# Storing normalized tokens in quarters: one edit in the input projection of a hybrid mixer kernel

## The chip, the cores and the metric

The kernel runs on one core of one Trainium2 chip. The metric is device time in microseconds (us) of one execution; a lower time is better. The core has TensorE (PE, matrix products; its weight loads are shown as PEld), VectorE (DVE), ScalarE (ACT), GpSimd (POOL) and SyncE (SP). SP computes nothing here: it issues nearly all DMA transfers, in the order of its own queue, and an issue whose data aren't ready holds everything that is queued behind it.

## What is computed

Two layers, each over 2048 latent tokens and 256 context tokens of width 1024. A layer normalizes its tokens, modulates them, projects them once for four parallel mixers (differential attention, an S5 state space model, a gated linear recurrence HGRN2, and multi-head latent attention), gates the mixers' outputs, projects them back and adds them to the residual:

```
shift, scale, gate = jnp.split(mod.astype(F32), 3, axis=-1)
h = (rms_norm(x) * (1.0 + scale) + shift).astype(dt)
(da_q, da_k, da_v, da_g, s5_u, s5_g, hg_q, hg_ff, hg_fb, hg_i, hg_g,
 mla_cq, mla_ckv, mla_kr, mla_g) = split_columns(h @ P["w_in"][l])
...
mixed = jnp.concatenate([a_out, b_out, c_out, d_out], axis=-1)
x = (x.astype(F32) + gate * (mixed @ P["w_out"][l]).astype(F32)).astype(dt)
```

All data are float32. `h`, the normalized tokens, is what this case is about.

## The kernel before, in words

A layer runs in three phases: the first stage, the mixers, and the output projection. The 2304 tokens (2048 latent, then 256 context) stand in the free dimension, the width in eight chunks of 128 partitions. Products of full precision are made of three passes over a high and a low part of each operand (`mm3`, lines 176 to 179): high times high, high times low, low times high.

The first stage of a layer is `proj1`, woven with `s5_build`, which works out the tables of the S5 mixer on GpSimd, VectorE and ScalarE and some on TensorE (`first_stage`). `proj1` cuts the tokens into six parts of 384. For each part `prep` (line 432) calls `h_block` (line 275): three token tiles are loaded, squared and summed on ScalarE, and for each of the eight chunks TensorE transposes and scales them (line 299), ScalarE writes the high part `hi` (line 304) and the unrounded value `t32` (line 305), and VectorE writes the low part `lo` as their difference (line 306). High and low part are tiles of 128 partitions by 8 chunks by 384 tokens, 1536 KB each. Parts 0, 2, 4 share one pair of buffers and parts 1, 3, 5 another.

`proj1` itself needs the parts only in those buffers. It multiplies them with five blocks of weights for attention keys and queries, and with value weights, and its evacuations (`evac1`, `store_qk` line 356, values line 501) store to memory: `KD` and `QD` take the keys and queries of differential attention, `KRD` the shared rotary key, `VT` the values. The second projection, `proj2`, works in blocks of 576 tokens, and loads `h` back from the tensor `HD` (line 522). `keep` (line 439) is what puts it there: one store of the whole high part and one of the whole low part (line 441).

`keep(0)` is called behind the loads of all weights, `keep(1)` behind the fourth block of weights of part 0, and every other one right after its `prep`. The program is written in this order, but a planner with durations of its own works out the order of each engine's queue and of SP's from it (`schedule_with_timeline_sim` in `TCKW`): instructions are placed when their operands are ready by its clock, the earlier written first. In layer 0 the first part is prepared while the modulation is worked out (`startup`), whose sixteen weight loads go through seven buffers.

The S5 build stores its tables `SC` (lines 1303 and 1312) and `ED` (line 1335) from the same SP queue. When it ends, its space goes to `proj2`, whose first four loads of `h` follow then.

Of the kernel before, what the change touches and what calls it, by code (L numbers as in the profile page):

```python
# [10 lines left out]
F32 = mybir.dt.float32  # L11
# [92 lines left out]
def run(g):  # L104
    for _ in g:
        pass


PR = (0, 0)
AVB = 2  # L110
PPB = 3
DA_A = 740
# [32 lines left out]
def pst(g, tag, name):  # L145
    if tag == "mm":
        tags = g.banks.get(name, g.banks["*"])
        g.rr[name if name in g.banks else "*"] += 1
        tag = tags[g.rr[name if name in g.banks else "*"] % len(tags)]
    return g.ps.tile([128, 512], F32, tag=tag, name=name, bufs=PSB[tag])  # L150


def pool(g, name, bufs, side="left"):
    return g.tc.tile_pool(name=name, bufs=bufs, side=side, reuse_waits="tile")
# [31 lines left out]
def rsqrt_col(g, pool, out, ss, inv_n, tag):  # L186
    nc = g.nc
    v = pool.tile([128, 1], F32, tag=tag + "v", name=tag + "v")
    nc.vector.tensor_scalar(v, ss, inv_n, EPS, ALU.mult, ALU.add)
    nc.gpsimd.tensor_tensor(out, v, g.mhalf, ALU.pow)  # L190
# [78 lines left out]
def x_src(g, l, tok):  # L269
    if l == 0:  # L270
        return g.A["x_s"][tok:tok + 128] if tok < LS else g.A["x_p"][tok - LS:tok - LS + 128]
    return g.X1[tok:tok + 128]


def h_block(g, l, tok0, n, p, hi, lo, mod):
    nc = g.nc
    xs, ds = [], []
    for t in range(n // 128):
        xt = p.tile([128, D], F32, tag="xt", name="xt", bufs=3)
        nc.sync.dma_start(xt, x_src(g, l, tok0 + t * 128))  # L280
        ss = p.tile([128, 1], F32, tag="ss", name="ss")
        junk = p.tile([128, D], BF16, tag="junk", name="junk", bufs=1)
        nc.scalar.activation(out=junk, in_=xt, func=AF.Square, accum_out=ss)
        r = p.tile([128, 1], F32, tag="r", name="r")
        rsqrt_col(g, p, r, ss, 1.0 / D, "rs")
        dg = p.tile([128, 128], F32, tag="dg", name="dg", bufs=4)
        nc.vector.tensor_scalar(dg, g.ident, r, None, ALU.mult)
        xs.append(xt)
        ds.append(dg)
    cut = min(max(LS - tok0, 0), n)  # L290
    if mod is not None:
        next(mod)
    for kc in range(8):
        if mod is not None and kc % 2 == 0:
            next(mod)
            next(mod)
        ps = pst(g, "mm", "pst")
        for t in range(n // 128):
            nc.tensor.matmul(ps[:, t * 128:(t + 1) * 128], lhsT=xs[t][:, kc * 128:(kc + 1) * 128], rhs=ds[t], start=True, stop=True)
        t32 = p.tile([128, 384], F32, tag="t32", name="t32")  # L300
        for a, b, gr in ((0, cut, 0), (cut, n, 1)):
            if b > a:
                sc, sh = g.scale[:, gr, kc:kc + 1], g.shift[:, gr, kc:kc + 1]
                nc.scalar.activation(out=hi[:, kc, a:b], in_=ps[:, a:b], func=AF.Identity, bias=sh, scale=sc)
                nc.scalar.activation(out=t32[:, a:b], in_=ps[:, a:b], func=AF.Identity, bias=sh, scale=sc)
        nc.vector.tensor_tensor(lo[:, kc, :], t32, hi[:, kc, :].bitcast(F32), ALU.subtract)
    if mod is not None:
        run(mod)

# [111 lines left out]
def proj1(g, l):  # L421
    nc = g.nc
    N = 384
    with ExitStack() as es:
        px = es.enter_context(pool(g, "pjx", 2))
        ph0 = es.enter_context(pool(g, "pjh0", 1))
        pw0 = es.enter_context(pool(g, "pjw0", 1))
        pws = es.enter_context(pool(g, "pjs", 2))
        starts = list(range(0, NT, N))
        hs = {}  # L430

        def prep(i):
            ph = ph1 if i % 2 else ph0
            hi = ph.tile([128, 8, N], F32R, tag="hhi", name="hhi")
            lo = ph.tile([128, 8, N], F32R, tag="hlo", name="hlo")
            h_block(g, l, starts[i], N, px, hi, lo, mod if i == 0 else None)
            hs[i] = (hi, lo)

        def keep(i):
            for part, x in enumerate(hs[i]):  # L440
                nc.sync.dma_start(g.HD[part, :, :, starts[i]:starts[i] + N], x.bitcast(F32))

        mod = startup(g) if l == 0 else None
        pw = es.enter_context(pool(g, "pjw", 1))
        prep(0)
        ph1 = es.enter_context(pool(g, "pjh1", 1))
        p = es.enter_context(pool(g, "pj", 2))
        wf = []

        def load_f(k):  # L450
            m = len(FB1[k][2])
            w32 = pws.tile([128, 8, 128], F32, tag="w32", name="w32")
            q = pw0 if k == 0 else pw
            hi = q.tile([128, 8, 128], F32R, name=f"wfh{k}")
            lo = q.tile([128, 8, 128], F32R, name=f"wfl{k}")
            nc.sync.dma_start(w32[:, :, :m], g.A["wF"][l, k] if m == 128 else g.A["wFp"][l])
            split2(g, hi[:, :, :m], lo[:, :, :m], w32[:, :, :m], "act", "vec" if k == 0 else W1LO)
            wf.append((hi, lo))

        load_f(0)  # L460
        if l == 0:
            late_consts(g)
        for k in range(1, len(FB1)):
            load_f(k)
        wth = pw.tile([128, 8, 512], F32R, name="wth")
        wtl = pw.tile([128, 8, 512], F32R, name="wtl")
        for kc in range(0, 8, 2):
            w32 = pws.tile([128, 2, 512], F32, tag="w32", name="wt32")
            nc.sync.dma_start(w32, g.A["wT"][l, :, kc:kc + 2, :])
            split2(g, wth[:, kc:kc + 2, :], wtl[:, kc:kc + 2, :], w32, "act", W1LO)  # L470
        keep(0)
        yield
        cache_keys(g, l, p)
        for i, tok0 in enumerate(starts):
            if 0 < i < len(starts) - 1:
                prep(i + 1)
                keep(i + 1)
            if i == 2 and l == 0:
                for rows in [g.KRD[0, 32:34]] + [g.KD[i, 96:98] for i in range(8)]:
                    nc.sync.dma_start(rows.rearrange("o (a b) -> (o a) b", b=128), g.ones[0:2 * NK // 128, :])  # L480
            hi, lo = hs.pop(i)
            rope_tables(g, p, tok0, N)
            for k, (kind, idx, cols) in enumerate(FB1):
                if i == 0 and k == H1:
                    prep(1)
                    keep(1)
                m = len(cols)
                ps = pst(g, "mm", "psF")
                for kc in range(8):
                    mm3(nc, ps[:m, :N], wf[k][0][:, kc, :m], wf[k][1][:, kc, :m], hi[:, kc, :], lo[:, kc, :], kc == 0, kc == 7)  # L490
                evac1(g, l, p, kind, idx, ps, tok0, N)
                yield
            for t in range(N // 128):
                ts_ = slice(t * 128, (t + 1) * 128)
                tok = tok0 + t * 128
                ps = pst(g, "mm", "psT")
                for kc in range(8):
                    mm3(nc, ps, hi[:, kc, ts_], lo[:, kc, ts_], wth[:, kc, :], wtl[:, kc, :], kc == 0, kc == 7)
                o = p.tile([128, 512], F32, tag="ev", name="evT")
                nc.scalar.copy(o, ps)  # L500
                (nc.gpsimd if i + 1 == len(starts) else nc.sync).dma_start(g.VT[tok:tok + 128, :], o)
                if tok >= LS:
                    nc.sync.dma_start(g.O["new_diff_v"][l, tok - LS:tok - LS + 128, :], o[:, 0:256])
                yield
# [261 lines left out]
def diff_attn(g, l, p, p1):  # L766
# [74 lines left out]
    def pass2(pr, qb):  # L841
# [20 lines left out]
        for ki, kt in enumerate(kts):  # L862
# [11 lines left out]
            late.append((ki, aa, last))  # L874
            if len(late) > AVB:
                av_mm(late[:AVB])
                del late[:AVB]
        g.kfree = max(g.kfree, 3 * pr + 3) if qb == QLAST else g.kfree
# [9 lines left out]
def mla(g, l, p):  # L888
# [47 lines left out]
    def pass2(pr, qb):  # L936
# [17 lines left out]
        for ki, kt in enumerate(kts):  # L954
# [18 lines left out]
            late.append((ki, e, last))  # L973
            if len(late) > AVB:
                av_mm(late[:AVB])
                del late[:AVB]
        g.kfree = max(g.kfree, 3 * (pr + 2) + 3) if qb == QLAST else g.kfree
# [455 lines left out]
def mixers(g, l):  # L1433
    with ExitStack() as es:
# [23 lines left out]
        with (g.tc.manual_schedule(engines={mybir.EngineType.PE}) if MAN else ExitStack()):  # L1458
            run(weave((att, 520 + 700 - DA_A), (ahead(g, ssm(), PR[1]), YW)))

# [145 lines left out]
def first_stage(g, l):  # L1606
    with pool(g, "sb1", 2, "right") as q1, pool(g, "sb", 1, "right") as qb:
        run(weave((proj1(g, l), 49), (s5_build(g, l, q1, qb), SBW)))
# [198 lines left out]
```

## Time and profile before

| | |
|---|---|
| median of 3 runs | 5268.16 us (5264.66 to 5270.53) |
| the profiled execution | 5276.37 us |
| its span in the trace | 5274.6 us |
| TensorE busy | 4733.3 us (90%) |
| VectorE busy | 3786.4 us (72%) |
| ScalarE busy | 3229.7 us (61%) |
| GpSimd busy | 1087.2 us (21%) |
| moved by DMA | 599.37 MB, mean 114 GB/s |

Busy time is the time in which an engine has an instruction under way. The profile is one execution, and its time is a little over the median of the timed runs, so that changes are worked out within it and then set against the median. The first stage of layer 0 lies at about 0 to 420 us of the span, that of layer 1 at about 2670 to 3060 us. The profile says for each instruction when it started, how long it took, and what it waited for.

### The profile page before, as it was taken

How to read it: one execution, taken by the hardware profiler on the slowest of the kernel's cores; microseconds unless marked ns; L12 is line 12 of the kernel's file. 1: busy time of each engine (PE TensorE's matmuls, PEld its weight loads, DVE VectorE, ACT ScalarE, POOL GpSimd, SP SyncE). 2: the span in 40 equal slices, each digit the busy share in tenths (PEclk: the TensorE clock that was granted, in tenths of full speed). 3: DMA queues.
4: the chain of work that ended last, by engine and by line, in shares of the span. 5: the costliest groups of instructions: out<-in, count | busy, mean ns of one | idle time of the engine just before them, and what ended most of it. 6: DMA issues, size and time to landing. Idle time of an engine off the chain costs nothing.

```text
span 5274.6 us, 81078 instructions
## 1 busy us (share of the span) xinstructions
PE 4733.3 (90%) x27920; PEld 3447.7 (65%) x27920; DVE 3786.4 (72%) x7468; ACT 3229.7 (61%) x7628; POOL 1087.2 (21%) x1323
## 2 busy tenths in 40 slices
PE   6887999999998998898988879999998989989899
PEld 5776767677665664456777757676776666654477
DVE  7645767676668886896676557676766678879876
ACT  4335878777777774235444268787777767733354
POOL 3751222222210000000228612222222100000022
PEclk8898999999998998899999979999999989989999
DMA  7455233433232124415445552325332321241353
GB/s 230 164 176 155 91 102 96 131 112 108 92 83 75 47 58 122 138 50 160 147 165 196 169 166 93 106 86 145 102 109 87 82 74 49 56 116 52 80 151 126
DMA packets 507523, 599.37 MB, mean 114 GB/s; under 512 B 147630, under 2 KB 414806, under 8 KB 507110
## 3 DMA queue, kind: packets, MB, share of 16 engines
q1 hardware_dynamic: 506630, 592.61, 37.5%
q8 instruction: 221, 3.62, 0.3%
q14 instruction: 192, 1.57, 0.1%
q0 software_dynamic: 480, 1.57, 0.1%
HBM read 378.42 MB, written 215.18 MB: 113 GB/s over the span
## 4 chain that ended last, share of the span: by engine, by line
PE 50%; DVE 18%; DMA 11%; ACT 10%; issue 5%; POOL 4%; SPq 2%; ACTq 0%; DVEq 0%; POOLq 0%
PE psav L858 5%; PE psS L870 4%; PE psF L177 4%; PE psF L178 4%; PE psF L179 4%; PE psS L817 4%; PE psmav L950 4%; ACT junk L820 3%; DVE nm L818 2%; PE psM L961 2%; DVE a L872 2%; PE psM L926 2%; PE pshg L1017 2%; ACT pp L871 2%; PE psM L963 2%
## 5 line engine op out<-in xcount | busy, mean ns | idle before, releaser
L818 DVE TENSOR_REDUCE nm<-psS 128x1 f32<-128x512 f32 (+1 forms) x1312 | 790.5, 627 | 358.6 <-PE psS L817 347.8
L820 ACT ACTIVATE junk<-psS,nm 128x512 bf16<-128x512 f32 (+1 forms) x1312 | 847.9, 646 | 207.9 <-DVE nm L818 188.6
L871 ACT ACTIVATE pp<-psS 128x512 f32<-128x512 f32 (+1 forms) x1184 | 653.5, 594 | 171.6 <-PE psS L870 165.6
L177 PE MATMUL psF<-h,whi 128*128 128x288 f32 x2304 | 699.5, 304 | 31.8 <-ACT whi L169 31.8
L872 DVE SCALAR_TENSOR_TENSOR a<-pp,nlam 128x512 f32<-128x512 f32 (+1 forms) x592 | 509.8, 863 | 259.1 <-ACT pp L871 258.5
L178 PE MATMUL psF<-h,whi 128*128 128x288 f32 x2304 | 689.6, 299 | 0.0
L179 PE MATMUL psF<-h,wlo 128*128 128x288 f32 x2304 | 686.6, 298 | 1.8 <-DVE wlo L173 1.8
L964 ACT ACTIVATE me<-psM 128x512 f32<-128x512 f32 (+1 forms) x592 | 344.7, 590 | 434.7 <-PE psM L963 389.2
L817 PE MATMUL psS<-ks,qs 96*128 96x512 f32 (+1 forms) x1312 | 544.9, 426 | 54.6 <-ACT junk L820 28.4
L870 PE MATMUL psS<-qs,ks 98*128 98x512 f32 (+1 forms) x1184 | 444.0, 440 | 57.5 <-ACT junk L820 45.0
L177 PEld LDWEIGHTS psF<-h,whi 128*128 128x128 f32 x2304 | 446.0, 194 | 64.4 <-ACT whi L169 33.4
L171 POOL CAST whi<-w 128x1024 fp32r<-128x1024 f32 x140 | 152.0, 1086 | 1625.3 <-PE psF L178 1287.0
L178 PEld LDWEIGHTS psF<-h,whi 128*128 128x128 f32 x2304 | 446.3, 194 | 54.5
L927 DVE TENSOR_REDUCE mnm<-psM 128x1 f32<-128x512 f32 (+1 forms) x656 | 394.7, 626 | 77.4 <-PE psM L926 75.8
L179 PEld LDWEIGHTS psF<-h,wlo 128*128 128x128 f32 x2304 | 442.9, 192 | 3.1 <-DVE wlo L173 3.1
L870 PEld LDWEIGHTS psS<-qs,ks 98*128 98x128 f32 x1184 | 205.9, 194 | 239.2 <-ACT junk L820 139.4
L817 PEld LDWEIGHTS psS<-ks,qs 96*128 96x128 f32 x1312 | 256.9, 198 | 159.1 <-ACT junk L820 87.8
L173 POOL TENSOR_TENSOR wlo<-w,whi 128x1024 fp32r<-128x1024 f32 x140 | 351.2, 2508 | 11.2
L967 DVE TENSOR_TENSOR macc<-macc,me 128x1024 f32<-128x1024 f32 x256 | 312.0, 1219 | 30.5 <-ACT me L964 29.1
L858 PE MATMUL psav<-a,dav 128*64 128x512 f32 (+1 forms) x1184 | 311.3, 648 | 18.4 <-DVE a L872 18.4
L950 PE MATMUL psmav<-me,mv 128*64 128x512 f32 (+1 forms) x1184 | 315.0, 629 | 9.8 <-ACT me L964 9.5
L1368 POOL MEMSET s5rt<- 128x2 f32 x16 | 1.6, 101 | 1511.3 <-ACT s5rt L1367 1511.3
(449 smaller groups left out, 10508.6 us busy)
## 6 DMA issues: line engine op xcount, KB each, us to landing
w<-wF SPq DMA_DIRECT2D x152, 512.0 KB
h<-HD SPq DMA_DIRECT2D x64, 576.0 KB
wmod<-w_mod SPq DMA_DIRECT2D x48, 512.0 KB
HD<-hhi SPq DMA_DIRECT2D x12, 1536.0 KB
HD<-hlo SPq DMA_DIRECT2D x12, 1536.0 KB
GX<-ev SPq DMA_DIRECT2D x128, 144.0 KB
gt<-GX SPq DMA_DIRECT2D x36, 512.0 KB
PF<-ev SPq DMA_DIRECT2D x96, 144.0 KB
```

The source lines that it names most:

```text
L177: nc.tensor.matmul(out, lhsT=w_hi, rhs=x_hi, start=start, stop=False)
L178: nc.tensor.matmul(out, lhsT=w_hi, rhs=x_lo, start=False, stop=False)
L179: nc.tensor.matmul(out, lhsT=w_lo, rhs=x_hi, start=False, stop=stop)
L817: nc.tensor.matmul(ps[:, :kn], lhsT=qs[0:96, i, t * 128:(t + 1) * 128], rhs=key_cols(ks[i], k0, kn)[0:96], start=True, stop=True)
L818: nc.vector.tensor_reduce(nm[:, i, t, ci:ci + 1], ps[:, :kn], axis=AX.X, op=ALU.max, negate=True)
L820: nc.scalar.activation(out=junk[:, :kn], in_=ps[:, :kn], func=AF.Exp, bias=nm[:, i, t, ci:ci + 1], accum_out=sm[:, i, t, ci:ci + 1])
L858: x = nc.tensor.matmul(av[hh * 64:(hh + 1) * 64, :n], lhsT=v[:, kt, hh * 64:(hh + 1) * 64], rhs=aa[:, hh, :n], start=(ki == 0), stop=(ki = ...
L870: nc.tensor.matmul(ps[:, :n], lhsT=key_cols(ks[2 * hh + m], kt * 128, 128), rhs=qs[:, 2 * hh + m, :n], start=True, stop=True)
L871: nc.scalar.activation(out=pp[:, m, :n], in_=ps[:, :n], func=AF.Exp)
L872: last = nc.vector.scalar_tensor_tensor(aa[:, hh, :n], pp[:, 1, :n], nlam, pp[:, 0, :n], ALU.mult, ALU.add)
L927: nc.vector.tensor_reduce(nm[:, i, t, ci:ci + 1], ps[:, :kn], axis=AX.X, op=ALU.max, negate=True)
L950: x = nc.tensor.matmul(av[i * 64:(i + 1) * 64, :n], lhsT=v[:, kts[ki], i * 64:(i + 1) * 64], rhs=e[:, i, :n], start=(ki == 0), stop=(ki == ...
```

## The change

`keep` goes. In its place, `h_block` issues two stores after every second chunk, one for the two chunks of the high part and one for those of the low part, so that a part is stored in four pieces of 384 KB for each of `hi` and `lo`. The writing of the high part by ScalarE (line 304) is the same in both kernels.

```
+HDP = 2
...
         nc.vector.tensor_tensor(lo[:, kc, :], t32, hi[:, kc, :].bitcast(F32), ALU.subtract)
+        if kc % HDP == HDP - 1:
+            k0 = kc + 1 - HDP
+            for part, x in enumerate((hi, lo)):
+                nc.sync.dma_start(g.HD[part, :, k0:kc + 1, tok0:tok0 + n], x[:, k0:kc + 1, :].bitcast(F32))
...
-        def keep(i):
-            for part, x in enumerate(hs[i]):
-                nc.sync.dma_start(g.HD[part, :, :, starts[i]:starts[i] + N], x.bitcast(F32))
...
-        keep(0)
         yield
         cache_keys(g, l, p)
...
                 prep(i + 1)
-                keep(i + 1)
...
                     prep(1)
-                    keep(1)
```

## Rows read from the trace of the kernel before

**Rows 1.** The page's head: span; busy us (share) and instructions of each engine.
```profile
span 5274.6 us, 81078 instructions
PE 4733.3 (90%) x27920; PEld 3447.7 (65%) x27920; DVE 3786.4 (72%) x7468; ACT 3229.7 (61%) x7628; POOL 1087.2 (21%) x1323
```

**Rows 2.** By windows: stretch, length, busy PE PEld DVE ACT POOL, PEclk, DMA share, GB/s.
```profile
120.00:360.00 240.00, 200.12 (x1016) 176.98 (x1015) 148.69 (x308) 86.27 (x193) 176.89 (x390) 0.93 0.49 160
2730.00:3000.00 270.00, 234.52 (x1218) 206.89 (x1219) 180.45 (x464) 110.51 (x239) 194.25 (x411) 0.96 0.54 181
```

**Rows 3.** Waits of TensorE, 0 to 480 us: us in total, times, longest.
```profile
PE pswz L1301 <- POOL wz L257: 12.1, 7, 3.2
...
PE pso L339 <- ACT x L373: 10.8, 1, 10.8
```

**Rows 4.** Issues on HD, whole span: count; ns min/median/max; first and last start.
```profile
L522 SPq DMA_DIRECT2D h<-HD x64: 370/506/3401, 363.5 to 3886.2; - x64
L441 SPq DMA_DIRECT2D HD<-hhi x12: 552/564/1247, 68.8 to 2970.8; - x12
L441 SPq DMA_DIRECT2D HD<-hlo x12: 785/1207/2906, 70.2 to 2975.4; - x12
```

**Rows 5.** Timeline of VectorE: start, us, instruction [idle before]; sixth and eighth low part.
```profile
343.81 0.58 DVE L306 TENSOR_TENSOR hlo<-t,hhi 128x384 fp32r<-128x384 f32 x1 [1.05 <-ACT t L305]
...
350.12 0.56 DVE L306 TENSOR_TENSOR hlo<-t,hhi 128x384 fp32r<-128x384 f32 x1 [0.71 <-ACT t L305]
```

**Rows 6.** Timeline of SP's queue, end of layer 0's first stage.
```profile
357.81 0.57 SPq L441 DMA_DIRECT2D HD<-hhi  x1
...
361.35 1.98 SPq L441 DMA_DIRECT2D HD<-hlo  x1
363.50 9.39 SPq L522 DMA_DIRECT2D h<-HD  x4
372.98 3.20 SPq L356 DMA_DIRECT2D QD<-sphi  x2
...
382.64 6.97 SPq L501 DMA_DIRECT2D VT<-evT  x3
```

**Rows 7.** By windows of 5 us, before and in that burst.
```profile
340.00:345.00 5.00, 5.00 (x34) 5.00 (x33) 3.46 (x7) 4.03 (x10) 3.19 (x11) 1.00 0.27 74
...
365.00:370.00 5.00, 5.00 (x24) 4.14 (x23) 0.00 (x0) 0.59 (x1) 0.00 (x0) 1.00 1.01 316
370.00:375.00 5.00, 5.00 (x30) 4.88 (x29) 0.55 (x1) 0.00 (x0) 0.00 (x0) 1.00 1.03 343
```

**Rows 8.** Timelines of ScalarE and TensorE behind the burst.
```profile
388.68 0.58 ACT L500 COPY evT<-psT 128x512 f32<-128x512 f32 x1 [22.78 <-DMA VT<-evT]
...
389.71 0.58 PE L339 MATMUL pso<-ident,x 128*128 128x128 f32 x1 [10.82 <-ACT x L373]
```

**Rows 9.** Timelines at the start of layer 1: ScalarE, VectorE (two), TensorE.
```profile
2726.50 0.40 ACT L169 CAST krhi<-kr 32x256 fp32r<-32x256 f32 x1 [3.41 <-DMA kr<-cmr]
...
2729.00 0.17 DVE L1196 TENSOR_TENSOR k<-ph 128x16 f32<-128x16 f32 x1
2729.20 0.42 DVE L173 TENSOR_TENSOR krlo<-kr,krhi 32x256 fp32r<-32x256 f32 x1
...
2730.26 0.64 PE L177 MATMUL psF<-hhi,wfh 128*96 128x384 f32 x1 [12.23 <-ACT x L373]
```

**Rows 10.** Chain of waits in order of time: start, us, what; two low query stores.
```profile
171.56 13.20 DMA QD<-splo
...
3042.59 12.27 DMA QD<-splo
```

**Rows 11.** By windows, the start of layer 0.
```profile
0.00:30.00 30.00, 16.36 (x167) 11.82 (x167) 10.85 (x42) 12.65 (x19) 5.15 (x9) 0.99 0.98 316
```

**Rows 12.** Waits of SP's queue, 60 to 420 us: us in total, times, longest.
```profile
SPq L1303 <- DVE so L1285: 26.3, 4, 14.0
...
SPq L441 <- ACT t L305: 8.9, 1, 8.9
```

## The prediction

> **What bounds the kernel now.** I read the page's head first: TensorE is busy 4733 of 5274.6 us [rows 1]. The change touches only the first stage of the two layers, so next come two wide stretches of the view by windows. In the two stretches where normalized tokens are prepared beside other work, TensorE is busy 200.1 of 240 us in layer 0 and 234.5 of 270 us in layer 1 [rows 2]: 39.9 + 35.5 = 75.4 us idle. That is all that anything here can win, outside the two starts and the hand-over to the second projection. The DMA share is only 0.49 and 0.54 in those stretches [rows 2]: the bytes fit, and what matters is when they come. The waits of TensorE name who ends its idle time: mostly the S5 build on GpSimd (the largest row of it 12.1 us, in 7 waits), and one wait of 10.8 us that a transfer stands behind [rows 3]. So the reader should look for places where the stores of normalized tokens stand ahead of something that is waited for, and not expect the whole idle time back.
>
> **What the change does, in counts.** Before, 12 stores of the high and 12 of the low part are issued, with a median of 0.56 and 1.21 us on the SP queue [rows 4], each of 1536 KB. Afterwards there are 96 of 384 KB: 72 issues more. Bytes and run lengths in memory stay the same (384 tokens in a row), so DMA time itself is costed at no change. No arithmetic is added: the high part is written by ScalarE in both kernels. A store of a quarter waits for its second low part only. In the sixth part of layer 0 the third quarter is complete after the sixth subtraction, at 343.81 + 0.58 = 344.4 us, and the last at 350.7 [rows 5]; but the two big stores were issued at 357.81 and 361.35 [rows 6]. Three quarters of 3072 KB, 2.36 MB, can leave the burst that forms there. At 316 to 343 GB/s, the rate of that burst [rows 7], this is 6.9 to 7.5 us of full DMA; I use 7.1.
>
> **Step 1, end of layer 0's first stage: -6 us.** Behind the two stores stand four loads of h, which hold SP from 363.50 for 9.4 us, then two query stores at 372.98 and, at 382.64, three value stores [rows 6]. The DMA share is 1.01 and 1.03 from 365 to 375 us, and 0.27 at 340 to 345 [rows 7]: room where the three quarters would go, and none where they are now. ScalarE waits 22.78 us for a value store to free its buffer, and TensorE stands 10.82 us behind it [rows 8]. Taking 7.1 us of transfers out, and paying two issues of 0.55 us for the last quarter, moves this chain by 6.0 us. Bounds: 0, if the value stores are held by the query stores alone, and 10.8, all of TensorE's wait. I take 6 since full DMA share reaches to the issue of the query stores.
>
> **Step 2, start of layer 1: 0.** There TensorE waits 12.23 us, and a small load that lies behind the two stores lands late: ScalarE casts it at 2726.50. But the subtraction after it runs on VectorE at 2729.20, 0.03 us after its predecessor there ended at 2729.17 [rows 9]. VectorE is late by itself; an earlier load only waits longer. Bounds: 0 and -2.3 us (2729.20 less 2726.90, if VectorE's order lets it pass).
>
> **Step 3, end of layer 1's first stage: -1 us.** No h loads follow so closely; I take 1 us, bounds 0 and -7.1 (the moved bytes).
>
> **Step 4, the eight preparations in between (parts 2 to 5, counted from one, of each layer): -7 us.** After each, a low query store is awaited. It took 13.20 us to land after such a burst, but also 12.27 us at 3042.59, when no store of normalized tokens had been issued for 67 us [rows 10, 4]. So the burst explains 0.9 us of it, times 8 is 7. The other bound is 7.1 us each, 57 in all, which stays under the idle 75.4; below nothing it is Rival A's price. I take the low end, for the row without the burst is the same kind of transfer.
>
> **Step 5, start of layer 0: +2.5 us.** In the first 30 us the DMA share is 0.98 at 316 GB/s [rows 11]. Quarters of the first part now leave there, 0.79 MB or 2.5 us each pair, ahead of modulation weights that are still to come; the old stores came after them, the first at 68.8 us [rows 4]. Bounds: 0, if those weights have slack, and +10 (four pairs, the second part's counted with them). I take one pair.
>
> **Step 6, issues: 0.** 72 times 0.55 us is 40 us of SP time, 3.3 us for each part. What hides it: SP itself waits, for instance 26.3 us in 4 waits for the S5 build's output [rows 12]. Without that cover it costs up to 3.3 us where SP is late, 40 us at most. A quarter's wait at the head of SP's queue holds what is queued behind: key, query and value stores, S5 stores and token loads. ScalarE and VectorE wait for the first three to reuse their buffers. Its bounds are 0 and the 8.9 us that the old store already held SP once [rows 12]; I take 0, since most old stores came out of a busy queue, not a waiting one.
>
> **Sum.** -6 + 0 - 1 - 7 + 2.5 + 0 = -11.5 us. The profiled execution took 5276.37 us (5274.6 of it the span), 8.2 us over the median of the three timed runs; it would come to 5264.9. Against the median, 5268.16 - 11.5 = 5256.7; I say 5256.5, which is 0.22% faster. About 0.2% (10.5 us) is what a measurement of this kernel can tell from no change.
>
> **A rule against the change.** The burst at 365 to 375 us holds the loads of h, of 576 KB each by the code, and reaches 316 to 343 GB/s [rows 7, 6], so pieces under 1 MiB needn't run slow when many are in flight. The Trainium skill, "DMA: Bandwidth & Descriptors", section "Measured (HBM→SBUF, 128 partitions, SWDGE, issued from GpSimd)", says the opposite for a DMA alone: batch to at least 1 MiB for three quarters of the peak, 138 GB/s at 64 KB. As an estimate by that page, some 250 GB/s at 384 KB instead of 330 would add about 37 us of DMA time, and by it the sum would be near +25 us. No row here shows a 384 KB store by itself.
>
> **Rivals.**
> A, slower: SP is held by quarters. SP issues in the order that a planner worked out with its own durations; a quarter put too early holds everything behind it. For it: the old store held SP 8.9 us at the first part, and an S5 store waits 26.3 us in 4 waits [rows 12]. Against it: in the sixth part SP issued the stores 7 us after the data was there. There are 3 new early places in each of 10 later parts, 30. If a hold of mean 0.8 us at each reaches the end, that is +24 - 11.5 = +12.5: 5280.7 us. It outweighs the gain from 11.5 / 30 = 0.38 us a place.
> B, no change: the change doesn't spread the stores. SP stands at another head (the S5 waits of rows 12) while quarters become ready, and they go out together as now; or step 1's chain is held by the query stores, whose landing is 12 us without any burst [rows 10]. Then -6 falls out and half of step 4: 5268.2 - 1 - 3.5 + 2.5 = 5266.2 us.
> C, more gain: the S5 build is fed earlier, and the middle parts give half their upper bound, 28 us instead of 7: 5268.2 - 32.5 = 5235.7 us. For it: 75.4 us of idle TensorE. Against it: the 12.27 us landing without a burst.
> D, small pieces are slow, as the page's rule has it: from rows, all 37.7 MB at 316 instead of 343 GB/s is 119 instead of 110 us, +9: 5265.7 us.
>
> **How the numbers follow.** Forecast 0.45 (own range 5248 to 5264, of which 0.28 under 5257.6 and 0.17 above); A 0.20; B 0.20; C 0.12; D 0.03. Faster: 0.28 + 0.12 = 0.40; same: 0.17 + 0.20 + 0.03 = 0.40; slower: 0.20. The range leaves out half of A and most of C: 5238 to 5283.
>
> **What would show it.** Step 1: the four h loads issued some 5 us earlier and TensorE's wait near 390 us shorter than 6 us, with quarters issued before 350. Step 2: TensorE's wait at layer 1's start still over 9 us. Step 4: the query stores still land in 11 to 13 us and TensorE's idle in the two stretches falls by under 10 us of 75. Rival A: SP waits at the new line that add up to over 20 us, with ScalarE's waits for stores grown. B: quarters issued back to back. C: idle in the stretches down by 25 us. I am wrong also if the planner moves other engines' work far from where it is now; then the stretches without any store of normalized tokens differ as well.

## The result: slower by 0.56%, and the profile after

The changed kernel takes 5298.97 us in the median of 4 executions (5286.29 to 5302.35), the kernel before 5267.92 us. The ratio is 1.0056, with a 95% interval of 1.0038 to 1.0075: 20 to 40 us more. The forecast was 5256.5 us, a gain, with a range up to 5283. The measured time lies above that range, and the change went the other way.

The profiled execution of the changed kernel took 5298.13 us. Its head, with TensorE as busy as before [rows 1] in a span that is 21.5 us longer:

```profile
span 5296.1 us, 81173 instructions
PE 4728.1 (89%) x27920; PEld 3443.8 (65%) x27920; DVE 3785.2 (71%) x7468; ACT 3227.9 (61%) x7628; POOL 1077.0 (20%) x1323
```

The two stretches of [rows 2] by windows (length, busy PE, PEld, DVE, ACT, POOL, PEclk, DMA share, GB/s). TensorE's idle time in them was to fall by some 7 us from 75.4; it is 47.7 + 55.0 = 102.7 us:

```profile
120.00:360.00 240.00, 192.27 (x984) 170.98 (x985) 139.54 (x305) 89.00 (x200) 179.14 (x403) 0.91 0.53 175
2730.00:3000.00 270.00, 214.98 (x1087) 186.49 (x1085) 160.79 (x403) 97.17 (x214) 179.88 (x402) 0.92 0.52 169
```

The stores themselves do what the change says. The issues on HD, against [rows 4], are 96 for 24, the first 40 us earlier:

```profile
L520 SPq DMA_DIRECT2D h<-HD x64: 360/499/2037, 384.8 to 3890.5; - x64
L311 SPq DMA_DIRECT2D HD<-hhi x48: 359/462/2652, 28.6 to 2981.0; - x48
L311 SPq DMA_DIRECT2D HD<-hlo x48: 359/426/3477, 30.3 to 2986.0; - x48
```

What TensorE waits for in layer 1's first stage (2640 to 3070 us; us in total, times, longest) is new. The wait for ScalarE at the layer's start, 12.23 us before [rows 9], has shrunk to 0.3. In its place are a wait of 13.6 us for VectorE in the preparation of a part, and 17 waits, 33.6 us together, for the tile `wz` that the S5 build writes on GpSimd:

```profile
PE pswz L1299 <- POOL wz L258: 24.8, 11, 5.5
PE pst L300 <- DVE ph L253: 13.6, 1, 13.6
PE pswz L1299 <- POOL wz L255: 8.8, 6, 3.1
...
PE psF L178 <- ACT x L378: 0.3, 1, 0.3
```

In the kernel before, the waits for `wz` in the same window are 13.9 us in 7 waits:

```profile
PE pswz L1301 <- POOL wz L254: 7.7, 3, 3.9
...
PE pswz L1301 <- POOL wz L257: 6.2, 4, 3.3
```

None of these instructions is in the diff. Setting the compiled orders of the two kernels side by side shows why they could move: of TensorE's 22164 instructions 6103 stand at another place in the queue, of VectorE's 7392 it is 3222, of ScalarE's 6259 it is 1622, of GpSimd's 1319 it is 828, of SP's 2442 (stores of tokens aside) it is 587. Places differ in both first stages, and also in the mixers of both layers, where no line was edited. The planner had other stores to place, and came to another order for the work near them and also for work far behind them.

### The profile page after: what moved, and what is told of

Read it like the earlier page. It is cut to its first block, busy times and chain, and to the rows that moved or that the text cites. A ratio compares the mean times of both kernels' runs of the same rounds, so it can differ in the third digit from the quotient of the medians.

```text
span 5296.1 us, 81173 instructions
## 1 busy us (share of the span) xinstructions
PE 4728.1 (89%) x27920; PEld 3443.8 (65%) x27920; DVE 3785.2 (71%) x7468; ACT 3227.9 (61%) x7628; POOL 1077.0 (20%) x1323
## 3 DMA queue, kind: packets, MB, share of 16 engines
q1 hardware_dynamic: 507782, 592.61, 37.3%
## 4 chain that ended last, share of the span: by engine, by line
PE 49%; DVE 17%; DMA 13%; ACT 10%; issue 4%; POOL 4%; SPq 2%; ACTq 0%; DVEq 0%; POOLq 0%
PE psav L856 5%; PE psS L868 4%; PE psF L178 4%; PE psF L180 4%; PE psF L179 4%; PE psS L815 4%; PE psmav L948 3%; ACT junk L818 3%; PE psM L959 2%; DVE nm L816 2%; DVE a L870 2%; PE psM L924 2%; ACT pp L869 2%; PE pshg L1015 2%; PE psM L960 2%
## 5 line engine op out<-in xcount | busy, mean ns | idle before, releaser
L925 DVE TENSOR_REDUCE mnm<-psM 128x1 f32<-128x512 f32 (+1 forms) x656 | 393.7, 623 | 77.1 <-PE psM L924 75.4
L959 PE MATMUL psM<-qs,ks 98*128 98x512 f32 (+1 forms) x592 | 271.6, 459 | 49.8 <-ACT me L962 23.1
```

The costliest lines, as they stand in the source:

```text
L925: nc.vector.tensor_reduce(nm[:, i, t, ci:ci + 1], ps[:, :kn], axis=AX.X, op=ALU.max, negate=True)
```

## Experiments: the stores and the order taken apart

So there were three theories. **A**: the new order of other work costs the time. **B**: SP is held by quarters that stand in its queue before their data is ready (Rival A of the prediction). **C**: more and smaller transfers cost it.

To separate them, kernels were built in which every engine's order is written out and forced, by adding a scheduling edge from each instruction to the next:

```diff
+        for a, b in zip(row, row[1:]):
+            g.tc.add_manual_dep(b, a.name, mybir.DependencyInfo(mybir.DependencyClass.NoSync, mybir.DependencyReason.DATA), reason="order")
```

`row` is a list of numbers for each engine. In the diffs below the lists are named: `F0`, `M0`, `F1`, `M1` are layer 0's first stage, its mixers and output projection, and the same of layer 1; `old` is the order of the kernel before, `new` that of the changed kernel, and `early` that of run x2_early. `QUARTERS` chooses quarters or whole stores for each layer. These kernels' line numbers are 1 to 10 higher than those of the changed kernel: `wz` is written at L257 and L260, and `pswz` at L1309.

All ratios are to the kernel before on the same chip; the last column is the ratio applied to 5268 us.

| run | median us | ratio, 95% interval | us against before |
|---|---|---|---|
| changed kernel | 5298.97 | 1.0056, 1.0038 to 1.0075 | +30 (20 to 40) |
| x1_pieces | 5267.04 | 1.0001, 0.9990 to 1.0011 | +1 (-5 to 6) |
| x2_early | 5268.86 | 0.9998, 0.9983 to 1.0013 | -1 (-9 to 7) |
| x3_order | 5338.93 | 1.0131, 1.0112 to 1.0150 | +69 (59 to 79) |
| x4_first | 5301.22 | 1.0068, 1.0048 to 1.0088 | +36 (25 to 46) |
| x5_layer0 | 5269.28 | 1.0011, 0.9997 to 1.0025 | +6 (-2 to 13) |
| x6_layer1 | 5282.18 | 1.0039, 1.0022 to 1.0056 | +21 (12 to 30) |
| x7_mixers | 5266.69 | 1.0004, 0.9990 to 1.0019 | +2 (-5 to 10) |
| x8_inblock | 5271.14 | 1.0012, 0.9997 to 1.0026 | +6 (-2 to 14) |
| x9_start | 5274.74 | 1.0023, 1.0009 to 1.0037 | +12 (5 to 19) |
| x10_build | 5280.62 | 1.0033, 1.0019 to 1.0047 | +17 (10 to 25) |
| x11_undo | 5286.60 | 1.0040, 1.0023 to 1.0057 | +21 (12 to 30) |
| c_before | 5262.07 | 1.0003, 0.9988 to 1.0017 | +2 (-6 to 9) |
| x12_build_noed | 5267.87 | 1.0012, 1.0000 to 1.0024 | +6 (0 to 13) |
| x13_early_noed | 5258.45 | 0.9988, 0.9974 to 1.0002 | -6 (-14 to 1) |
| x14_halves | 5295.50 | 1.0061, 1.0044 to 1.0077 | +32 (23 to 41) |
| x15_layer1_free | 5277.35 | 1.0026, 1.0015 to 1.0038 | +14 (8 to 20) |
| x16_build_nohd | 5246.53 | 0.9961, 0.9948 to 0.9975 | -21 (-27 to -13) |
| x17_early_nohd | 5248.74 | 0.9964, 0.9949 to 0.9979 | -19 (-27 to -11) |

**x1_pieces.** Quarters, in the old order, where the whole stores stood.

```diff
-QUARTERS = (False, False)
+QUARTERS = (True, True)
+ORDER = F0(old) + M0(old) + F1(old) + M1(old)
```

> Every engine keeps the order of instructions of the kernel before. Only the 24 whole stores of normalized tokens become 96 quarter stores, the four of a part standing where the whole one stood in SP's queue, so none leaves earlier than before. Theory A, the rest of the program stands in another order and that costs the time: about 5268 us, as before. Theory B, SP is held by quarters that stand in its queue before their data is ready: about 5268 us too, because here a quarter waits for nothing that the whole store did not wait for. Theory C, more and smaller transfers (96 for 24) cost the time by themselves: about 5299 us, as the changed kernel.

Measured: 5267.04 us, ratio 1.0001. Theory C falls: 72 more issues, and pieces of 384 KB, at the old places, cost nothing that can be measured.

**x2_early.** Quarters as early as the planner places them, but nothing else may move.

```diff
-QUARTERS = (False, False)
+QUARTERS = (True, True)
+ORDER = F0(old) + M0(old) + F1(old) + M1(old), quarters of tokens left free in SP's queue
```

> The quarters are issued early, where the planner puts them when it may, but every other instruction on every engine, SP's other issues included, keeps the order of the kernel before. Theory A (the new order of the other work costs the time): not above 5268 us, and if the sum of the prediction was right about the stores themselves, 5256 us. Theory B (SP is held by early quarters): about 5299 us, as the changed kernel. Theory C (small transfers): about 5299 us.

Measured: 5268.86 us, ratio 0.9998. Theory B in its plain form falls, and so does my sum for the stores: -1 us (-9 to 7) instead of -11.5. Rival A had asked to look for waits of SP at the new line, over 20 us of them. They are there in the changed kernel (whole span, us in total, times, longest): the two largest rows come to 46.6 us, all rows of the line to 72.6 us.

```profile
SPq L311 <- DVE hlo L307: 26.3, 15, 3.8
SPq L311 <- ACT hhi L305: 20.3, 13, 3.0
```

And here, where they cost nothing, the two largest come to 51.5 us and all to 82.6 us. As a sign they prove nothing:

```profile
SPq L312 <- ACT hhi L307: 31.5, 13, 9.1
SPq L312 <- DVE hlo L309: 20.0, 12, 3.5
```

The other half of that sign, longer waits of ScalarE for stores, went the other way. Up to 3100 us ScalarE waits 166 us for key, query and value stores in the kernel before and 148 us in c_before, but 99 us in x2_early and 77 us in the changed kernel, and neither of these is faster for it.

**x3_order.** The new order, with whole stores.

```diff
+ORDER = F0(new) + M0(new) + F1(new) + M1(new), whole store at its fourth quarter's place
```

> The opposite of the run before: every engine takes the order of the changed kernel, but the tokens go out as whole stores, each at the place of its fourth quarter in SP's queue. Theory A (the new order of the other work costs the time): 5299 us, give or take 10 us. Theories B and C (the quarters cost it): about 5268 us.

Measured: 5338.93 us, ratio 1.0131. It is slow without any quarter, as theory A has it, but 40 us slower than the changed kernel, which no theory expected. In the new order, then, quarters gain 40 us over whole stores at the places of the last quarters; in the old order they gain nothing. So theory A is not the whole of it: what the stores cost depends on the order. TensorE's waits for `wz` in layer 1's first stage (2640 to 3070 us) are 42 us here, 4 of them at L257:

```profile
PE pswz L1309 <- POOL wz L260: 38.0, 12, 12.1
```

## Experiments: where the new order costs

**x4_first, x5_layer0, x6_layer1, x7_mixers, x11_undo.** The new order in some of the four stretches only.

```diff
x4_first
+QUARTERS = (True, True)
+ORDER = F0(new) + M0(old) + F1(new) + M1(old)
x5_layer0
+QUARTERS = (True, False)
+ORDER = F0(new) + M0(old) + F1(old) + M1(old)
x6_layer1
+QUARTERS = (False, True)
+ORDER = F0(old) + M0(old) + F1(new) + M1(old)
x7_mixers
+QUARTERS = (False, False)
+ORDER = F0(old) + M0(new) + F1(old) + M1(new)
x11_undo
+QUARTERS = (True, True)
+ORDER = F0(new) + M0(new) + F1(early) + M1(new)
```

> The order of the changed kernel, quarters included, in the first stage of both layers; the order of the kernel before, on every engine, in the mixers and output projections of both layers, where the changed kernel has no edited line. Read from the traces, the changed kernel reached the end of layer 0's first stage 1.8 us earlier, gained 13.7 us more until layer 1's start, lost 17.8 us in layer 1's first stage, and 19.2 us after it. Theory A with each stretch independent of the others: 5268 - 2 + 18 = 5284 us. Theories B and C: what follows a first stage is disturbed by the stores alone, so about 5299 us.

> Order of the changed kernel, with its quarters, in the first stage of layer 0 alone; everything behind it has the order and the whole stores of the kernel before. The runs so far leave theory A (the new order of other work costs the time) and give some 33 us to the two first stages together. By the milestones of the traces layer 0's first stage cost nothing: 5266 us. If the loss is spread evenly over both first stages: 5284 us.

> Order of the changed kernel, with its quarters, in the first stage of layer 1 alone; all else as in the kernel before. By the milestones of the traces nearly all of the loss is here: 5286 to 5301 us. If it is spread evenly over both first stages: 5284 us. If the new order did no harm here: 5268 us.

> Whole stores and the order of the kernel before in both first stages; the order of the changed kernel in the mixers and output projections of both layers, where nothing of the change stands. By the milestones of the traces the new order gains 13.7 us in layer 0's mixers and loses 19.2 us in layer 1's: 5274 us. If these two were only scatter between executions: 5268 us.

> The changed kernel, quarters and all, with only layer 1's first stage put back into the old order (that of the run with early quarters). Theory A with the loss in that stage, by the run with the new order there alone (+17 us): 5299 - 17 = 5282 us; by the changed kernel's time less layer 0's +4 and the mixers' +2: 5274 us. If the loss comes from the whole program and not from this stage: 5299 us.

Measured: 5301.22, 5269.28, 5282.18, 5266.69 and 5286.60 us. The two first stages hold the whole loss (x4: +36). Layer 1's has most of it (x6: +21), layer 0's at most 13 (x5: +6), the mixers nothing that can be measured (x7: +2). These three add up to 29 of the changed kernel's 30. Putting layer 1's first stage back (x11) wins about 9, less than the 21 that it costs alone, though the intervals meet.

The expectations for x4 and x7 had read a gain of 13.7 us in layer 0's mixers and a loss of 19.2 us in layer 1's out of one trace of each kernel. Their sum, +5.5 us, can't be told from the +2 of x7_mixers, so neither the gain nor the loss is shown or refuted. From layer 0's first product of attention to layer 1's first token load, x7_mixers takes 2224.3 us, like the changed kernel, where the kernel before takes 2238.2 us; but x3_order, with the same order there, takes 2247.1 us.

**c_before.** The kernel before, its own order forced.

```diff
+ORDER = F0(old) + M0(old) + F1(old) + M1(old)
```

> The kernel before, with its own order written out and forced on every engine: a second trace of the same instructions in the same order, to see how far the milestones of one execution differ from another's. All theories: 5268 us; milestones within the spread of its times, some 10 us.

Measured: 5262.07 us. Between this trace and the first one of the same order the span differs by 14.6 us (5260.0 and 5274.6). Of this, 9.7 us arise before layer 0's first product of attention, which starts at 419.3 us here and at 429.0 us in the first trace, so a milestone of one trace is good to some 10 us. The length of a stage that holds the same work repeats better in these two: 2238.0 and 2238.2 us from there to layer 1's first token load, 393.8 and 393.7 us from that load to layer 1's first product of attention. TensorE's waits for `wz` in layer 1's first stage are 14.4 us in 7 waits here, 16.6 us in 9 in x2_early, and 33.6 us in 17 in the changed kernel.

```profile
PE psF L180 <- ACT x L380: 12.2, 1, 12.2
...
PE pswz L1309 <- POOL wz L257: 8.8, 3, 3.7
...
PE pswz L1309 <- POOL wz L260: 5.6, 4, 2.7
```

**x9_start, x10_build.** Layer 1's first stage cut in two at the point where the S5 build sets in; all else as in x2_early.

```diff
x9_start
+QUARTERS = (True, True)
+ORDER = F0(early) + M0(early) + F1(new up to the S5 build, then early) + M1(early)
x10_build
+QUARTERS = (True, True)
+ORDER = F0(early) + M0(early) + F1(early up to the S5 build, then new) + M1(early)
```

> Quarters everywhere. The order is that of the run with early quarters and the old order, except at the start of layer 1's first stage (its weights, the preparation of its first three parts, up to where the S5 build on GpSimd sets in): there it is the changed kernel's. Of TensorE's instructions 298 stand elsewhere. The waits of TensorE in the changed kernel name two suspects in this stage: one wait of 13.6 us for VectorE in the preparation of a part, and 17 waits, 33.6 us together, for the S5 build on GpSimd, where the kernel before has 7 waits and 13.9 us. If the start is what costs: 5268 + 14 to 20 = 5282 to 5288 us. If the S5 build's place costs it: 5268 us.

> The other part of the same stage: the changed kernel's order from where the S5 build sets in to the end of layer 1's first stage, the old order before and after; quarters everywhere. If the S5 build's place among TensorE's other work is what costs: 5282 to 5288 us, and TensorE's waits for GpSimd grow to some 30 us here. If the start costs it: 5268 us.

Measured: 5274.74 and 5280.62 us. Both parts cost: +12 (5 to 19) for the start, +17 (10 to 25) for the build. Together that is 29 us where x6_layer1 had 21 (12 to 30), which the intervals allow. In x9_start the wait for VectorE is back (12.7 us, 2640 to 2800 us) and ScalarE's wait of 12.2 us is gone from the place that it has in x2_early, so the start changes one wait for another, and the traces don't show where its 12 us arise:

```profile
PE pst L302 <- DVE ph L255: 12.7, 1, 12.7
```

In x10_build the waits for `wz` grow to 35.5 us (2640 to 3070 us). GpSimd itself waits 43.5 us (2750 to 3010 us) until its own stores, issued for it from SP's queue, have freed their buffers: the tables `Eb` and the blocks `so`:

```profile
PE pswz L1309 <- POOL wz L260: 24.0, 11, 7.1
...
PE pswz L1309 <- POOL wz L257: 11.5, 6, 5.2
...
POOL Eb L1339 <- DMA ED<-Eb: 31.6, 6, 10.3
POOL so L1288 <- DMA SC<-so: 11.9, 4, 6.0
```

The same four lines of x2_early give 16.6 and 26.3 us:

```profile
PE pswz L1309 <- POOL wz L260: 9.5, 6, 3.9
PE pswz L1309 <- POOL wz L257: 7.1, 3, 4.4
...
POOL Eb L1339 <- DMA ED<-Eb: 20.7, 5, 10.0
POOL so L1288 <- DMA SC<-so: 5.6, 2, 4.4
```

## Experiments: why the new order costs in the S5 build

**x12_build_noed, x13_early_noed.** Layer 1's stores of the S5 tables left out, in the order of x10_build and in that of x2_early.

```diff
-            nc.sync.dma_start(g.ED[i, :, gs], Eb[i])
+            if l == 0:
+                nc.sync.dma_start(g.ED[i, :, gs], Eb[i])
```

> The order of the run with the new order around the S5 build (5280.6 us), with layer 1's 16 stores of the S5 tables (ED from Eb) left out, so that layer 1 reads layer 0's tables. GpSimd waits 31.6 us in 6 waits for these stores in that run and 20.7 us in 5 waits in the old order. If these waits are why TensorE waits for GpSimd in the new order: the time falls by the 11 to 12 us that the new order costs, and TensorE's waits for the S5 build fall from 35.5 to about 17 us. If it is not these waits, but how GpSimd's and TensorE's work are put side by side: the new order stays 12 us slower than its control, the next run.

> The control of the run before: early quarters and the old order (5268.9 us), with the same 16 stores of layer 1 left out. If the waits for these stores are what costs in the new order, this and the run before are equal within 5 us; if not, this one is about 12 us faster. By itself it should lie between 5257 us (half of the 20.7 us of GpSimd's waits reach the end) and 5269 us (none does).

Measured: 5267.87 and 5258.45 us. Leaving these stores out gains 11 us in the new order (+17 to +6) and in the old one 5 us (-1 to -6), which can't be told from nothing; the new order stays 9.4 us behind. The tables' stores alone are not the cause: with them gone, GpSimd waits for the other kind, 25.4 us in the new order,

```profile
POOL so L1288 <- DMA SC<-so: 25.4, 7, 13.5
```

and 6.3 us in the old:

```profile
POOL so L1288 <- DMA SC<-so: 6.3, 2, 5.1
```

The difference, 19 us, is about what it was with both kinds there (43.5 - 26.3 = 17). But GpSimd's waits for its own stores do not sort the runs: in the same window they are 33.3 us in the kernel before, 31.9 us in c_before and 32.9 us in x6_layer1, which is 21 us slower.

**x16_build_nohd, x17_early_nohd.** The stores of layer 1's tokens left out instead, in the same two orders.

```diff
-        if QUARTERS[l] and kc % 2 == 1:
+        if l == 0 and kc % 2 == 1:
```

> The order of the run with the new order around the S5 build (5280.6 us), with all 48 stores of layer 1's normalized tokens left out, so that layer 1's second projection reads layer 0's tokens. In that order GpSimd waits 43.5 us for its own stores on SP's queue (tables 31.6, blocks 11.9), in the old order 26.3 us (20.7 and 5.6). If it is the quarters, in the places that the new order gives them ahead of those stores, that make GpSimd wait: its waits fall to some 26 us, and the time comes within 5 us of its control, the next run. If it is the order of the other work: it stays some 12 us slower than its control, with GpSimd's waits near 43 us.

> The control: early quarters and the old order (5268.9 us), with the same 48 stores of layer 1 left out. If the quarters delayed GpSimd's stores in the new order only: 5264 to 5269 us, as with them. If the tokens' stores cost time in any order: below 5264 us by what they cost.

Measured: 5246.53 and 5248.74 us. Without the token stores the two orders can't be told apart, so around the S5 build no cost of the new order by itself is measured; one below some 10 us could hide. In the new order these stores cost 17 + 21 = 38 us (x10 to x16), in the old 18 us (x2 to x17), each good to some 10 us. GpSimd's waits for its own stores fall from 43.5 to 16.1 us in the new order, and TensorE's for `wz` from 35.5 to 26.7 us:

```profile
PE pswz L1309 <- POOL wz L260: 18.7, 11, 4.8
...
PE pswz L1309 <- POOL wz L257: 8.0, 5, 3.5
...
POOL Eb L1339 <- DMA ED<-Eb: 9.9, 5, 5.9
POOL so L1288 <- DMA SC<-so: 6.2, 1, 6.2
```

In the old order they fall from 26.3 to 11.1 us, and from 16.6 to 11.9 us:

```profile
PE pswz L1309 <- POOL wz L260: 6.0, 5, 2.7
PE pswz L1309 <- POOL wz L257: 5.9, 4, 2.4
...
POOL Eb L1339 <- DMA ED<-Eb: 11.1, 1, 11.1
```

The length of the stage says where this arises. From layer 1's first token load to its first product of attention every run has the same TensorE work (1637 or 1638 recorded instructions). By windows (length, busy PE, PEld, DVE, ACT, POOL, PEclk, DMA share, GB/s), the kernel before, x2_early, x10_build, the changed kernel, x16_build_nohd and x17_early_nohd:

```profile
2667.20:3060.90 393.70, 320.09 (x1638) 281.12 (x1636) 238.80 (x678) 144.16 (x298) 224.85 (x455) 0.93 0.56 187
2652.30:3052.10 399.80, 322.86 (x1637) 284.75 (x1635) 242.07 (x678) 144.75 (x298) 224.80 (x455) 0.92 0.57 184
2662.00:3068.50 406.50, 327.03 (x1637) 284.35 (x1635) 237.62 (x678) 145.46 (x298) 217.16 (x455) 0.92 0.55 181
2651.70:3059.90 408.20, 328.31 (x1638) 285.76 (x1636) 241.03 (x678) 145.86 (x298) 218.59 (x455) 0.91 0.55 180
2658.40:3032.10 373.70, 315.86 (x1638) 273.96 (x1636) 244.50 (x678) 145.38 (x298) 223.14 (x455) 0.96 0.44 145
2652.80:3030.10 377.30, 317.75 (x1637) 279.73 (x1636) 243.96 (x678) 144.69 (x298) 229.04 (x455) 0.94 0.45 146
```

In the seven traces with the old order and all stores in this stage it takes 393.7 to 403.6 us, in the five with the changed kernel's order in all of it or from the S5 build on, 406.5 (x10_build) to 427.3 us (x3_order). Without the token stores it is 32.8 us shorter in the new order (x10 to x16) and 22.5 us in the old (x2 to x17), so their price arises here. The waits for `wz` are a poor measure of that price. From x2_early to x10_build they grow by 18.9 us and the stage by 6.7 us, as other waits of TensorE shrink (for `cp` at L257 from 12.7 to 4.2 us). In x16_build_nohd they are 14.8 us longer than in x17_early_nohd, and the stage is 3.6 us shorter. And of the 14.5 us by which the changed kernel's stage is longer than before, 8.2 us are busy time of the same TensorE work, at a mean granted clock of 0.91 instead of 0.93.

So what is shown is this: in layer 1's first stage the token stores cost time, and more of it in the new order than in the old. That they do it through GpSimd's late stores and TensorE's waits for GpSimd is not shown. Whether they do it by their places in SP's queue or by the bytes that they move is open too, since leaving a store out takes away both.

## Experiments: other orders from the planner

**x8_inblock, x14_halves, x15_layer1_free.** Nothing forced. Whole stores issued inside the preparation; halves; quarters in layer 1 alone.

```diff
x8_inblock
-        if QUARTERS[l] and kc % 2 == 1:
+        if QUARTERS[l] and kc % 8 == 7:
...
x14_halves
-        if QUARTERS[l] and kc % 2 == 1:
+        if QUARTERS[l] and kc % 4 == 3:
...
x15_layer1_free
-QUARTERS = (False, False)
+QUARTERS = (False, True)
```

> Nothing is forced. The two whole stores of a part are issued inside the preparation, after the last piece, not after it returns: as many stores, as large, waiting for the same data; only those of each layer's first part stand earlier in the program, ahead of the weights' loads. The planner all the same puts 3504 of TensorE's 22164 instructions at other places. Theory A: the time is that of another order, which can differ from 5268 us by some 10 to 30 us to either side, and quarters are not needed for that. Theories B and C: 5268 us, within 0.2%.

> Nothing is forced. Two stores a part and half instead of four quarters (48 for 24), each issued as soon as its half is there. The planner puts another 4 to 5 thousand of TensorE's 22164 instructions elsewhere than before, and not where the quarters made it put them. Theory A: the time is that of this order and has no reason to lie between the kernel before and the changed one: anywhere from 5260 to 5310 us, and TensorE's waits for the S5 build in layer 1's first stage tell which (some 15 us as before, or some 35 us as in the changed kernel). Theories B and C: between the two, about 5283 us.

> Nothing is forced. Quarters in layer 1 alone, so that layer 0 keeps the whole stores and, by the planner, its old order; 1375 of TensorE's instructions stand elsewhere, nearly all in layer 1's first stage. Theory A: as the run with the changed kernel's order there, 5280 us, if the planner comes to a like order without layer 0's quarters, and TensorE then waits some 35 us for the S5 build; about 5268 us if TensorE's waits for it stay near 15 us. Theories B and C: half of the loss, 5283 us.

Measured: 5271.14, 5295.50 and 5277.35 us. Time doesn't go with the number of stores: 48 halves (x14_halves) cost as much as 96 quarters, and the 60 stores of x15_layer1_free cost 14 us where the 96 of x2_early cost nothing. x8_inblock, with 24 whole stores and 3504 moved instructions of TensorE, is 6 us slower at an interval that takes in no change: an order can move far and cost little. TensorE's waits for `wz` in layer 1's first stage are 26.1 us in x14_halves and 30.9 us in x15_layer1_free. They don't go with the loss in size: 26.1 us at +32, 30.9 at +14. Nor is the loss of x14_halves in that stage, which is 398.1 us long:

```profile
2682.80:3080.90 398.10, 329.17 (x1638) 285.64 (x1636) 242.99 (x678) 144.95 (x298) 220.37 (x455) 0.92 0.55 183
```

Its layer 1 begins late instead: the first token load starts at 2682.8 us, against 2650 to 2667 us in the traces that have layer 0 in the old order.

## Why the prediction was wrong, step by step

**The step that failed** is one that the sum does not have. Its six steps move the stores and leave every other instruction where it was. That the planner might move other engines' work stood in the last sentence before the forecast line, without a price, a chance or a rival of its own. Measured, it is the whole result: the stores alone are worth -1 us (x2_early), the stores with the order that the planner made for them +30. The stretches that were to show it did: the changed kernel's mixers, too, have another order, though no cost of that part can be measured (x7_mixers). How the order costs is known only in part. The sum also took the bytes of the stores to fit, at a DMA share of 0.49 and 0.54. But in the old order, too, layer 1's 48 token stores cost 18 us (x2_early to x17_early_nohd), by their bytes or by their places.

**Step 1 (-6)** moved the right chain, by less than it said and without gain. SP's queue at the end of layer 0's first stage in x2_early, to be set beside [rows 6]:

```profile
343.24 2.47 SPq L363 DMA_DIRECT2D QD<-sphi  x2
345.81 2.73 SPq L312 DMA_DIRECT2D HD<-hhi  x1
...
350.74 0.86 SPq L312 DMA_DIRECT2D HD<-hlo  x1
351.78 7.96 SPq L530 DMA_DIRECT2D h<-HD  x4
359.84 3.06 SPq L363 DMA_DIRECT2D QD<-sphi  x2
...
369.51 6.96 SPq L509 DMA_DIRECT2D VT<-evT  x3
```

In c_before, the nearer trace of the old order, the same chain runs

```profile
345.85 1.10 SPq L363 DMA_DIRECT2D QD<-sphi  x2
347.05 0.57 SPq L448 DMA_DIRECT2D HD<-hhi  x1
...
352.79 10.96 SPq L530 DMA_DIRECT2D h<-HD  x4
363.86 3.15 SPq L363 DMA_DIRECT2D QD<-sphi  x2
...
373.41 6.97 SPq L509 DMA_DIRECT2D VT<-evT  x3
```

Counted from the pair of query stores at its head, the value stores come after 26.3 us instead of 27.6. That is 1.3 us, not 6, though three quarters of each part had left before: the loads of `h` still hold SP for 8 us. And the wait of TensorE behind this chain, which was to be shorter than 6 us, is 10.4 us in x2_early and 9.5 us in c_before (300 to 440 us):

```profile
PE pso L346 <- ACT x L380: 10.4, 1, 10.4
PE pso L346 <- ACT x L380: 9.5, 1, 9.5
```

In the changed kernel the planner put those loads behind the query stores, at 384.75, and there the wait is 4.9 us.

**Step 2 (0)** held in the old order: TensorE's wait there is 12.2 us in x2_early as in c_before. **Step 3 (-1)** can't be told from zero. **Step 4 (-7)** was near in the stretches: TensorE's idle time in them, 75.4 us [rows 2], is 510 - 442.4 = 67.6 us in x2_early. But the old order gives 72.3 us in c_before and 77.2 us in x1_pieces, the end did not come earlier, and the landing that was to shorten did not: the low query store that follows layer 1's last token stores lands in 12.8 us in x2_early, against 11.9 us in the kernel before and 12.0 us in c_before. **Step 5 (+2.5)** can't be checked closely: in the first 120 us TensorE is busy 78.5 us in x2_early, and 80.4 to 83.3 us in three traces of the old order. **Step 6 (0)** was right: x1_pieces prices 72 more issues at +1 us (-5 to 6).

**Rival A** named slower, and held SP as the cause. Its sign, SP's waits at the new line, was there and meant nothing (x2_early). Its mechanism, stores of tokens that delay what stands with them on SP's queue, may be part of what the stores cost in layer 1's first stage (38 us in the new order, 18 in the old, for the stores as a whole), but no run parts it from the cost of their bytes. What decided was the order, which Rival A did not have. **Rival B**, no change, was right of the stores alone in its number, 5266.2 us, but not in its first reason: the quarters do go out spread. **Rival C**'s gain did not come: idle time in the stretches was to fall by 25 us. In the new order quarters beat whole stores by 40 us (x3_order), but no run shows that the S5 build is the reason. **Rival D** is wrong: x1_pieces. By the estimate worked out there from the Trainium skill, "DMA: Bandwidth & Descriptors", section "Measured (HBM→SBUF, 128 partitions, SWDGE, issued from GpSimd)", pieces of 384 KB should have added some 37 us of DMA time. They added none: the packets of the DMA queue take 37.3% of the span of 5266.9 us in x1_pieces and 37.4% of 5260.0 us in c_before, 1965 and 1967 us, and the kernel's time moved by +1 us (-5 to 6).

**What stays open**: the start of layer 1's first stage (+12) and layer 0's (+6, which could be nothing) are placed, not explained. Why the token stores cost more in the new order is not known, and x11_undo fits the sum of the parts only within its interval. No order that was tried with quarters beats the kernel before.

## What to carry to other kernels

Where a planner works out the queues, an edit of a few lines is two changes, the lines and a new order, and the second can be the larger; set the compiled orders side by side before any sum is made, and give the order a rival with a price. Force the old order with the new lines, and the new order with the old lines, to learn which of the two a measured time belongs to; here the one gave -1 us and the other +69. A wait at a new line has no price until a run shows who is late behind it. Compare two traces by the length of a stage that holds the same instructions, not by one kind of wait or one milestone.

## What was not expected of the hardware

Two traces of one order differ by 14.6 us in their span (5274.6 and 5260.0), half of what was to be explained, so the spans of two traces could not have settled this. GpSimd waited up to 13.5 us at a time for a buffer whose store had to be issued from SP's queue, and when one kind of these stores was left out, its waits for the other grew from 11.9 to 25.4 us. Leaving out layer 1's 48 stores of tokens gave 18 us even in the old order, at a DMA share of about a half [rows 2] that the forecast had read as room enough.
